# Wide and narrow products on TensorE: three narrow products a weight tile in place of one wide and one narrow, new score order and pads in the attention phase

## Chip, cores and metric

The kernel runs on one core of a Trainium2 chip. The metric is the device time of one execution in microseconds; the time before is the median of three runs. The core's engines are TensorE (PE; its weight loads are shown as PEld), VectorE (DVE), ScalarE (ACT), GpSimd (POOL) and SyncE (SP, which issues the loads).

## What is computed

A decoder trunk of two layers on `x` of 256 positions by 2048 features, float32. Layer 0 is a sliding-window attention with 32 query heads and 8 key/value heads of 64 features, norms of q and k over the head, and a learned sink per head. Layer 1 is a recurrent block (RG-LRU). Each is followed by a gated MLP with a causal depthwise convolution (FFN) of 6144 hidden features.

```python
for layer in range(DEPTH):
    h = rmsnorm(x, mix_norm[layer])
    if layer % N_MIXERS == 0:
        x = x + sliding_window_attention(h, attn_w_qkv[j], attn_q_gain[j], attn_k_gain[j], attn_sinks[j], attn_w_o[j])
    else:
        x = x + rglru_block(h, rec_w_in[j], ..., rec_w_out[j])
    h = rmsnorm(x, ffn_norm[layer])
    x = x + conv_ffn(h, ffn_w_up[layer], ffn_conv_w[layer], ffn_conv_b[layer], ffn_w_down[layer])
```

`conv_ffn` is `u = dwconv(h @ w_up)`, split into `g` and `v`, then `(gelu(g) * v) @ w_down`. `rglru_block` projects by `w_in` to two halves, convolves one, forms two gates from it by block-diagonal matrices, runs a linear recurrence over positions, multiplies by gelu of the other half and projects by `w_out`.

## The kernel before

Everything is transposed: features lie on the 128 partitions, the 256 positions along the free axis (`T = 256`, `KD = 16` tiles of features). All weights come in chunks of 128 x 2048 float32 (1 MB), 376 of them, in one order fixed in `order`: 4 for k, 4 for v, 16 for q, 16 for wo, then FFN 0 (two halves, each 48 chunks up and 24 down), 32 for the recurrent projections `px` and `py`, 16 for the output projection, FFN 1. A chunk is 16 weight tiles of 128 x 128.

**Precision.** Products run in float32r. To keep float32 accuracy, each operand is split in two, high and low. A weight chunk gets `hi` (a rounded copy by ACT, `split_hi`, line 118) and `lo` (the rest, by DVE, `split_lo`, line 126). An activation tile holds both parts side by side: `h[:, k, 0, :]` high, `h[:, k, 1, :]` low, 256 columns each; `g`, `ao`, `z` and `xc` are made likewise. A product needs hi by x-high, hi by x-low and lo by x-high.

**Wide and narrow.** A PSUM bank holds 512 columns. A *wide* product multiplies a `hi` tile with both parts at once, 512 columns, so the left half of the bank gathers hi by x-high and the right half hi by x-low. A *narrow* product multiplies a `lo` tile with x-high, 256 columns, into the right half. A chunk is 16 wide and 16 narrow products. The consumer adds the halves: in the FFN ACT copies the left half (`ua`, line 738), DVE adds the right (`us`, line 739) and multiplies by the norm's factor (line 740); `projected` does the same in the recurrent stage (lines 810 to 812); the residual update `x_epi` takes two adds (lines 234, 235), and `q_epi` a copy, an add, then cast, square and subtraction (lines 514 to 518).

**Order of the products.** `products` (line 213) issues for each chunk a counted run of wide products, some left over from the chunk before, then the chunk's 16 narrow ones. The counts come from `counts` (line 223): 14, 16, 18 at a stage's head, then 15, 15, 18 over and over, and at a stage's end all that is left. `mm_hi` and `mm_lo` (lines 190 to 199) issue 16 wide and 16 narrow in turn: so in the recurrent projections, the attention phase and `late_pair`, the first two chunks behind a norm.

**Queues.** `advance` issues the next chunk's load on SP (three raw buffers), then `split_hi` on ACT and `split_lo` on DVE; the code places it behind each chunk's products, between the steps of the previous tile's epilogue (`step`, `finish`). Each engine works its queue in the order written.

**Attention rounds.** `attend(j)` issues query tile j's products in pieces, and between them, in this order: the values product of tile j-3 (`O`, nine narrow products, line 605), the scores of tile j-1 (`scores`, line 521) and the transposes of tile j-2's probabilities in two halves of three (line 587). `scores` issues first the four float32 products that sum the squares of q (line 527, which need `qsq`), then for the second block of queries four products of 512 columns (mask by an identity, then hi by low, low by high, hi by high: lines 533 to 536), then four of 256 for the first block. `wo` begins with three tiles d = 0 to 2 that are interleaved with the last rounds; their update `wo_epi` follows at line 698. d = 3 to 15 run as plain chunks through `products`.

**Addresses.** A pool lays its tiles out in the order in which they are first asked for, at multiples of 32 bytes a partition. By the tiles' sizes, `hi` and `lo` start 64 bytes past a multiple of 512 and `h`, `g`, `ao`, `z`, `xc`, `kz` and `vh` 128 past. The gates' weights `ghi` and `glo` start 128 past, `identr`, `maskr`, the transposed probabilities `pt` and the query tiles `qh` 32 past.

Of the kernel before, what the change touches and what calls it, by code (L numbers as in the profile page):

```python
# [19 lines left out]
F32 = mybir.dt.float32  # L20
# [20 lines left out]
def trunk(ctx, tc, xT, wq, wk, wv, wo, win, wg, wout, wup, wdn, mixg, ffng, kqg, sinks,  # L41
# [158 lines left out]

    left = []

    def hi_items(ps, hi, rhs, ks, off=0, n=P, start=True):
        return [[ps, hi[:, off + k * n:off + k * n + P], rhs[:, xk].rearrange("p a t -> p (a t)"),
                 start and k == ks[0][0], False] for k, xk in ks]

    def lo_items(ps, lo, rhs, ks, off=0, n=P, stop=True):
        return [[ps[:, T:], lo[:, off + k * n:off + k * n + P], rhs[:, xk, 0, :], False,  # L210
                 stop and k == ks[-1][0]] for k, xk in ks]

    def products(high, low, count):

        run = left + high
        count = len(run) if count is None else count
        left[:] = run[count:]
        if left and low[-1][4]:
            low[-1][4], left[-1][4] = False, True
        for ps, w, r, start, stop in run[:count] + low:  # L220
            pe.matmul(ps, lhsT=w, rhs=r, start=start, stop=stop)  # L221

    def counts(n):

        c = ([14, 16, 18] + [15, 15, 18] * (n // 3))[:n]
        c[-1] = None
        return iter(c)

    def x_epi(ps, d, n, gains, tp, out_=None, tag="xt"):

        t = tp.tile([P, n, T], F32, tag=tag, name=f"xt{st['use']}")
        xs = x[:, d:d + n, :]
        for i in ([slice(0, n)] if out_ is None else [slice(i, i + 1) for i in range(n)]):
            dve.tensor_tensor(out=t[:, i], in0=ps[:, i, 0:T], in1=xs[:, i], op=ALU.add)  # L234
            dve.tensor_tensor(out=xs[:, i], in0=ps[:, i, T:], in1=t[:, i], op=ALU.add)  # L235
            if out_ is not None:
                nc.sync.dma_start(out=out_[:, d:d + n, :][:, i], in_=xs[:, i])
# [76 lines left out]
    with ExitStack() as ph:  # L314
# [6 lines left out]

        kz = ap_.tile([P, 4, 2, 2, T], F32R, name="kz")
        vh = ap_.tile([P, 2, 2, 512], F32R, name="vh")
        ao = ap_.tile([P, KD, 2, T], F32R, name="ao")
# [4 lines left out]
        cb = ap_.tile([P, T], F32, name="cb")  # L329
# [3 lines left out]
        rcv = ap_.tile([P, 2], F32, name="rcv")  # L333
        bones = ap_.tile([P, P], F32, name="bones")
        ident = ap_.tile([P, P], F32, name="ident")
        identr = ap_.tile([P, P], F32R, name="identr")
        maskf = a2.tile([P, 2, T], F32, tag="pt", padded_shape=[P, 2, 768], name="maskf")
        maskr = ap_.tile([P, 2, T], F32R, name="maskr")
# [170 lines left out]
        def q_epi(j, ps):  # L509
            a = a2.tile([P, T], F32, tag="ka", name=f"qa{j}")  # L510
            s = a2.tile([P, T], F32, tag="ks", name=f"qs{j}")
            sq = a2.tile([P, T], F32, tag="ksq", name=f"qsq{j}")
            ql = a2.tile([P, 2, T], F32R, tag="qh", name=f"qh{j}")
            act.copy(out=a, in_=ps[:, 0:T])
            dve.tensor_tensor(out=s, in0=ps[:, T:], in1=a, op=ALU.add)
            act.copy(out=ql[:, 0, :], in_=s)
            act.activation(out=sq, in_=s, func=AF.Square)
            dve.tensor_tensor(out=ql[:, 1, :], in0=s, in1=f(ql[:, 0, :]), op=ALU.subtract)
            qs[j] = (ql, sq)

        def scores(j):
# [4 lines left out]
            for b in range(2):  # L526
                pe.matmul(pq[:, 2 * b:2 * b + 2], lhsT=sq[:, b * P:b * P + P], rhs=bones[:, 0:P:HD],
                          start=True, stop=True)
            for b, o, keys in ((1, S[:, 0:512].rearrange("p (a t) -> p a t", a=2), slice(0, T)),
                               (0, S[:, 512:768].rearrange("p (a t) -> p a t", a=2), slice(0, P))):  # L530
                tb = slice(b * P, b * P + P)
                mk = slice(0, T) if b else slice(P, T)
                pe.matmul(o, lhsT=identr, rhs=maskr[:, :, mk], start=True, stop=False)
                pe.matmul(o, lhsT=ql[:, 0, tb], rhs=kz[:, p, 1, :, keys], start=False, stop=False)
                pe.matmul(o, lhsT=ql[:, 1, tb], rhs=kz[:, p, 0, :, keys], start=False, stop=False)
                pe.matmul(o, lhsT=ql[:, 0, tb], rhs=kz[:, p, 0, :, keys], start=False, stop=True)
# [80 lines left out]
        def attend(j, ps, hi, lo, rhs, nk, fin=None):  # L617


            sm = None  # L620
            dma_next()
# [11 lines left out]
            mm_hi(ps, hi, rhs, rng(8, 10), start=False)  # L633
            if j >= 2:
                transposes(j - 2, 0)
            mm_hi(ps, hi, rhs, rng(10, 13), start=False)
            if j >= 2:
                transposes(j - 2, 1)
            mm_hi(ps, hi, rhs, rng(13, nk), start=False)
# [3 lines left out]
            mm_lo(ps, lo, rhs, rng(0, nk), stop=nk == KD)  # L643
# [20 lines left out]
        head = []  # L664
# [387 lines left out]
```

## Time and profile before

| | |
|---|---|
| median of 3 runs | 2178.98 us (2178.93 to 2179.07) |
| the profiled execution | 2179.0 us, of which span 2177.2 us |
| products on PE | 12676, busy 2162.8 us |
| DVE, ACT, POOL busy | 72%, 54%, 7% |
| HBM read | 401.06 MB, 185 GB/s over the span |

The profile is of one execution. Its page gives busy time by engine, a chain of work followed back from the last instruction, and groups of instructions by line with busy time, mean duration and the idle time ahead of them. Its other views are the waits, each with who ended it, and the timeline, in which equal instructions that follow each other form one row: start, duration, engine, line, operation, tiles, shape and count. A product's own duration is its way through the array and overlaps with the next one's. The pace at which products follow each other is read from the starts. `pu`, `pd`, `pr`, `px`, `py`, `pq`, `po` are the PSUM tiles of the FFN's up and down products, the output projection, the recurrent projections, the queries and wo.

### The profile page before, as it was taken

The numbers are of one execution on the slowest core, as the hardware profiler recorded it, in microseconds if no ns is written. First come the engines' busy times: TensorE is split into PE (matmuls) and PEld (weight loads), VectorE is DVE, ScalarE is ACT, GpSimd is POOL, SyncE is SP. The second block draws the span as 40 slices with busy tenths as digits, with TensorE's granted clock in tenths as the row PEclk, the third lists the DMA queues.
The fourth block names the chain that finished last, engine by engine and source line by source line (L and its number), as shares of the span: only waits on it lengthen the run. The fifth ranks groups of instructions, "written<-read, shape, count | busy, mean of one in ns | idle before, by whom it ended". The sixth has DMA issues, their size and how long they took to land.

```text
span 2177.2 us, 30752 instructions
## 1 busy us (share of the span) xinstructions
PE 2162.8 (99%) x12676; PEld 1899.5 (87%) x12676; DVE 1567.5 (72%) x1882; ACT 1174.0 (54%) x1432; POOL 143.6 (7%) x125
## 2 busy tenths in 40 slices
PE   9999999999999999999999999999999999999999
PEld 7878888888888888888888988888888888888888
DVE  6778777777654777776679877777776457777654
ACT  6777445555433555553369874555554335555432
POOL 1222220000000000002200003200000000000000
PEclk9999999999999999999999999999999999999999
DMA  7223555555555555555555546555555555555553
GB/s 274 104 102 112 193 188 199 195 192 194 193 193 194 185 192 191 191 193 195 189 213 186 191 151 214 185 196 194 192 192 196 188 186 191 193 192 193 192 195 135
DMA packets 60763, 405.14 MB, mean 186 GB/s; under 512 B 7504, under 2 KB 9936, under 8 KB 12880
## 3 DMA queue, kind: packets, MB, share of 16 engines
q1 hardware_dynamic: 60336, 403.04, 52.0%
q8 instruction: 99, 1.62, 0.3%
q14 instruction: 40, 0.33, 0.0%
q10 hardware_dynamic: 288, 0.15, 0.0%
HBM read 401.06 MB, written 2.10 MB: 185 GB/s over the span
## 4 chain that ended last, share of the span: by engine, by line
PE 94%; ACT 3%; DVE 2%; issue 1%; DMA 0%; SPq 0%; DVEq 0%; ACTq 0%
PE pu L221 47%; PE pd L221 24%; PE pr L221 4%; PE po L221 3%; PE py L192 3%; PE px L192 3%; PE px L198 1%; PE py L198 1%; PE pq L192 1%; ACT pr L565 1%; ACT hi L118 1%; PE pu L192 1%; PE pq L198 1%; DMA x<-in_xT 0%; PE po L192 0%
## 5 line engine op out<-in xcount | busy, mean ns | idle before, releaser
L126 DVE TENSOR_TENSOR lo<-raw,hi 128x2048 fp32r<-128x2048 f32 (+1 forms) x390 | 863.1, 2214 | 299.6 <-ACT hi L118 299.5
L118 ACT CAST hi<-raw 128x2048 fp32r<-128x2048 f32 x373 | 712.9, 1912 | 493.4 <-PE pd L221 220.8
L221 PE MATMUL pu<-h,hi 128*128 128x512 f32 x3008 | 719.1, 391 | 0.0
L221 PEld LDWEIGHTS pu<-h,hi 128*128 128x128 f32 x3008 | 551.0, 188 | 107.6
L221 PEld LDWEIGHTS pu<-h,lo 128*128 128x128 f32 x3008 | 369.7, 188 | 16.1
L221 PE MATMUL pu<-h,lo 128*128 128x256 f32 x3008 | 372.4, 276 | 0.0
L221 PE MATMUL pd<-g,hi 128*128 128x512 f32 x1536 | 367.3, 391 | 0.0
L221 PEld LDWEIGHTS pd<-g,hi 128*128 128x128 f32 x1536 | 281.4, 188 | 55.0
L221 PEld LDWEIGHTS pd<-g,lo 128*128 128x128 f32 x1536 | 188.9, 188 | 8.2
L221 PE MATMUL pd<-g,lo 128*128 128x256 f32 x1536 | 190.3, 276 | 0.0
L747 DVE SCALAR_TENSOR_TENSOR uy<-us,fw,uy 128x255 f32<-128x255 f32 (+1 forms) x384 | 176.6, 481 | 6.8
L754 ACT CAST g<-us 128x256 fp32r<-128x256 f32 x96 | 39.1, 407 | 246.2 <-DVE us L753 246.2
L739 DVE TENSOR_TENSOR us<-pu,ua 128x512 f32<-128x512 f32 x96 | 66.4, 691 | 88.9 <-ACT ua L738 88.8
L744 ACT ACTIVATE uy<-us,fb,fw 128x256 f32<-128x256 f32 x192 | 105.1, 599 | 2.7 <-DVE us L740 2.7
L738 ACT COPY ua<-pu 128x512 f32<-128x512 f32 x96 | 56.4, 587 | 77.6 <-PE pu L221 77.6
L192 PE MATMUL pq<-h,hi 128*128 128x512 f32 x256 | 73.7, 405 | 0.0
L755 DVE TENSOR_TENSOR g<-us,g 128x256 fp32r<-128x256 f32 x96 | 40.9, 426 | 45.4 <-ACT g L754 45.4
L740 DVE TENSOR_TENSOR us<-us,rb 128x512 f32<-128x512 f32 x96 | 66.4, 692 | 3.3
L161 POOL TENSOR_TENSOR sqa<-x 128x512 f32<-128x512 f32 x3 | 6.9, 2300 | 897.5 <-DVE x L235 897.5
L192 PE MATMUL px<-h,hi 128*128 128x512 f32 x256 | 61.8, 392 | 0.0
L192 PE MATMUL py<-h,hi 128*128 128x512 f32 x256 | 61.3, 392 | 0.0
L234 DVE TENSOR_TENSOR xt<-pd,x 128x512 f32<-128x512 f32 (+1 forms) x40 | 23.3, 582 | 50.3 <-PE pd L221 50.3
(226 smaller groups left out, 1925.7 us busy)
## 6 DMA issues: line engine op xcount, KB each, us to landing
raw<-in_wup SPq DMA_DIRECT2D x192, 1024.0 KB, 4.8
raw<-in_wdn SPq DMA_DIRECT2D x96, 1024.0 KB, 4.8
raw<-in_win SPq DMA_DIRECT2D x32, 1024.0 KB, 4.9
raw<-in_wq SPq DMA_DIRECT2D x16, 1024.0 KB, 4.8
raw<-in_wo SPq DMA_DIRECT2D x16, 1024.0 KB, 4.8
raw<-in_wout SPq DMA_DIRECT2D x16, 1024.0 KB, 4.7
raw<-in_wv SPq DMA_DIRECT2D x4, 1024.0 KB, 5.7
graw<-in_wg SPq DMA_DIRECT2D x8, 512.0 KB, 3.4
```

What stands on the lines that cost most here:

```text
L118: act.copy(out=his[c], in_=raws[c])
L126: dve.tensor_tensor(out=los[c][:, part], in0=raws[c][:, part], in1=f(his[c][:, part]), op=ALU.subtract)
L192: pe.matmul(ps, lhsT=hi[:, off + k * n:off + k * n + P], rhs=rhs[:, xk].rearrange("p a t -> p (a t)"), start=start and k == ks[0][0], stop ...
L198: pe.matmul(ps[:, T:], lhsT=lo[:, off + k * n:off + k * n + P], rhs=rhs[:, xk, 0, :], start=False, stop=stop and k == ks[-1][0])
L221: pe.matmul(ps, lhsT=w, rhs=r, start=start, stop=stop)
L738: act.copy(out=a, in_=ps[:, :, 0:T])
L739: dve.tensor_tensor(out=s, in0=ps[:, :, T:], in1=a, op=ALU.add)
L740: dve.tensor_tensor(out=s, in0=s, in1=rbb, op=ALU.mult)
L744: act.activation(out=y[:, i, :], in_=s[:, i, :], func=AF.Identity, scale=fw[:, layer, n, 2:3], bias=fb[:, layer, n:n + 1])
L747: dve.scalar_tensor_tensor(out=y[:, i, tap:], in0=s[:, i, 0:T - tap], scalar=fw[:, layer, n, 2 - tap:3 - tap], in1=y[:, i, tap:], op0=ALU. ...
L754: act.copy(out=g[:, m, 0, :], in_=s[:, 0, :])
L755: dve.tensor_tensor(out=g[:, m, 1, :], in0=s[:, 0, :], in1=f(g[:, m, 0, :]), op=ALU.subtract)
```

## The change

Outside the products behind k and v and `late_pair`, the wide product goes: each `hi` tile is multiplied with x-high and with x-low in two narrow products, and both, like the `lo` tile's, go into the left half of the bank. `two_hi` issues the 32 narrow products of a chunk's `hi` tiles, `one_lo` the 16 of its `lo` tiles. The consumers read one half: no copy and add in `q_epi`, one add in `x_epi`, only the multiply in `up_epi` and `projected` (through `whole`).

At the head of a stage, `begin(n)` keeps n chunks in the old form: 15 wide products each (those left over first), then the chunk's 16 narrow ones; behind the last of them what is left is issued as narrow halves. n is 3 for wo from d = 3, for each down half and for the recurrent projections, and 4 for each up half and the output projection. The tiles of these chunks are still joined from two halves.

`scores` now issues the second block's scores as two groups of four narrow products, one per head of the pair, then the squares' sums, then the first block's four; in each group low by high comes last. In the attention pool the small tiles move ahead of `vh`, and pads are put between; with them `vh`, `identr` and `qh` start 64 bytes past a multiple of 512 and `ao`, `maskr` and `pt` 128 past, with the tag `ks` gone. In the gates' pool pads of 448 and 64 bytes put `ghi` and `glo` at 64 and leave `xc` at 128.

```diff
+    def two_hi(ps, hi, rhs, ks, off=0, n=P, start=False):
+        for k, xk in ks:
+            for part in range(2):
+                pe.matmul(ps, lhsT=hi[:, off + k * n:off + k * n + P], rhs=rhs[:, xk, part, :],
+                          start=start and (k, part) == (ks[0][0], 0), stop=False)
+    def one_lo(ps, lo, rhs, ks, off=0, n=P, stop=True):
+        for k, xk in ks:
+            pe.matmul(ps, lhsT=lo[:, off + k * n:off + k * n + P], rhs=rhs[:, xk, 0, :], start=False,
+                      stop=stop and k == ks[-1][0])
+    def thirds(ps, hi, lo, rhs, ks, off, n, start, stop):
+        two_hi(ps, hi, rhs, ks, off, n, start)
+        one_lo(ps, lo, rhs, ks, off, n, stop)
+    head = {"n": 0, "left": []}
+    def begin(n):
+        head["n"] = n
+    def chunk(*items):
+        if not head["n"]:
+            for ps, *rest in items:
+                thirds(ps[:, 0:T], *rest)
+            return False
+        head["n"] -= 1
+        high, low = list(head["left"]), []
+        for ps, hi, lo, rhs, ks, off, n, start, stop in items:
+            for k, xk in ks:
+                w = slice(off + k * n, off + k * n + P)
+                high.append((ps, hi[:, w], rhs, xk, start and k == ks[0][0], stop))
+                low.append((ps, slice(T, 2 * T), lo[:, w], rhs[:, xk, 0, :], False, stop))
+        ops = [(ps, slice(0, 2 * T), w, rhs[:, xk].rearrange("p a t -> p (a t)"), first, stop)
+               for ps, w, rhs, xk, first, stop in high[:15]] + low
+        left = high[15:]
+        if not head["n"]:
+            ops += [(ps, slice(part * T, part * T + T), w, rhs[:, xk, part, :], False, stop)
+                    for ps, w, rhs, xk, first, stop in left for part in range(2)]
+            left = []
+        head["left"] = left
...
+        return True
...
+    def whole(s, ps, tp, two, name):
+        rbb = rb.unsqueeze(1).to_broadcast([P, 2, T])
+        if two[0]:
+            i = slice(0, 1 + two[1])
+            a = tp.tile([P, 2, T], F32, tag="a", bufs=1, name=name)
+            act.copy(out=a[:, i], in_=ps[:, i, 0:T])
+            dve.tensor_tensor(out=s[:, i], in0=ps[:, i, T:], in1=a[:, i], op=ALU.add)
+            dve.tensor_tensor(out=s[:, i], in0=s[:, i], in1=rbb[:, i], op=ALU.mult)
+        if not two[1]:
+            i = slice(int(two[0]), 2)
+            dve.tensor_tensor(out=s[:, i], in0=ps[:, i, 0:T], in1=rbb[:, i], op=ALU.mult)
...
     def x_epi(ps, d, n, gains, tp, out_=None, tag="xt", two=False):
...
-            dve.tensor_tensor(out=t[:, i], in0=ps[:, i, 0:T], in1=xs[:, i], op=ALU.add)
-            dve.tensor_tensor(out=xs[:, i], in0=ps[:, i, T:], in1=t[:, i], op=ALU.add)
+            if two:
+                dve.tensor_tensor(out=t[:, i], in0=ps[:, i, T:], in1=xs[:, i], op=ALU.add)
+            dve.tensor_tensor(out=xs[:, i], in0=ps[:, i, 0:T], in1=t[:, i] if two else xs[:, i], op=ALU.add)
...
         def q_epi(j, ps):
...
-            act.copy(out=a, in_=ps[:, 0:T])
-            dve.tensor_tensor(out=s, in0=ps[:, T:], in1=a, op=ALU.add)
-            act.copy(out=ql[:, 0, :], in_=s)
-            act.activation(out=sq, in_=s, func=AF.Square)
-            dve.tensor_tensor(out=ql[:, 1, :], in0=s, in1=f(ql[:, 0, :]), op=ALU.subtract)
+            act.copy(out=ql[:, 0, :], in_=ps[:, 0:T])
+            act.activation(out=sq, in_=ps[:, 0:T], func=AF.Square)
+            dve.tensor_tensor(out=ql[:, 1, :], in0=ps[:, 0:T], in1=f(ql[:, 0, :]), op=ALU.subtract)
...
         def scores(j):
...
-            for b in range(2):
-                pe.matmul(pq[:, 2 * b:2 * b + 2], lhsT=sq[:, b * P:b * P + P], rhs=bones[:, 0:P:HD],
-                          start=True, stop=True)
-            for b, o, keys in ((1, S[:, 0:512].rearrange("p (a t) -> p a t", a=2), slice(0, T)),
-                               (0, S[:, 512:768].rearrange("p (a t) -> p a t", a=2), slice(0, P))):
+            for b, o, m, kk in ((1, S[:, 0:256], maskr[:, 0], (0, slice(0, T))),
+                                (1, S[:, 256:512], maskr[:, 1], (1, slice(0, T))),
+                                (0, S[:, 512:768].rearrange("p (a t) -> p a t", a=2), maskr[:, :, P:],
+                                 (slice(0, 2), slice(0, P)))):
                 tb = slice(b * P, b * P + P)
...
+                pe.matmul(o, lhsT=identr, rhs=m, start=True, stop=False)
+                pe.matmul(o, lhsT=ql[:, 0, tb], rhs=kz[:, p, 1, kk[0], kk[1]], start=False, stop=False)
+                pe.matmul(o, lhsT=ql[:, 0, tb], rhs=kz[:, p, 0, kk[0], kk[1]], start=False, stop=False)
+                pe.matmul(o, lhsT=ql[:, 1, tb], rhs=kz[:, p, 0, kk[0], kk[1]], start=False, stop=True)
+                if kk[0] == 1:
+                    for c in range(2):
+                        pe.matmul(pq[:, 2 * c:2 * c + 2], lhsT=sq[:, c * P:c * P + P], rhs=bones[:, 0:P:HD],
+                                  start=True, stop=True)
...
         def attend(j, ps, hi, lo, rhs, nk, fin=None):
...
-            mm_hi(ps, hi, rhs, rng(0, 4))
+            two_hi(ps, hi, rhs, rng(0, 2), start=True)
             if j >= 3:
                 ao_split(j - 3, values(j - 3))
-            mm_hi(ps, hi, rhs, rng(4, 8), start=False)
+            two_hi(ps, hi, rhs, rng(2, 6))
             if 1 <= j <= 16:
                 S = scores(j - 1)
...
-            mm_lo(ps, lo, rhs, rng(0, nk), stop=nk == KD)
+            one_lo(ps, lo, rhs, rng(0, nk), stop=nk == KD)
...
+                if n == 0:
+                    gw.tile([P, 112], F32, name="gpad0")
                 hi = gw.tile([P, 1024], F32R, tag="ghi", name=f"ghi{n}")
                 lo = gw.tile([P, 1024], F32R, tag="glo", name=f"glo{n}")
+                if n == 0:
+                    gw.tile([P, 16], F32, name="gpad1")
```

More of the change, by code (lines that the diff above doesn't have):

```diff
@@ L780, in ffn @@
                         ks = [(kk, 8 * c + kk) for kk in range(8)]
-                        high, low = [], []
-                        for i in range(2):
-                            high += hi_items(ps[:, i], hi, g, ks, off=i * P, n=2 * P, start=c == 0)
-                            low += lo_items(ps[:, i], lo, g, ks, off=i * P, n=2 * P, stop=c == 2)
-                        products(high, low, next(runs))
+                        two = chunk(*((tiles[i], hi, lo, g, ks, i * P, 2 * P, c == 0, c == 2) for i in range(2)))
                         step(pend)
```

154 lines of the change are left out of this document (67 added, 87 removed).

## The prediction

> **What bounds the kernel.** I read the page first: busy shares, granted clock, chain.
>
> ```profile
> span 2177.2 us, 30752 instructions
> PE 2162.8 (99%) x12676; PEld 1899.5 (87%) x12676; DVE 1567.5 (72%) x1882; ACT 1174.0 (54%) x1432; POOL 143.6 (7%) x125
> ...
> PEclk9999999999999999999999999999999999999999
> ...
> PE 94%; ACT 3%; DVE 2%; issue 1%; DMA 0%; SPq 0%; DVEq 0%; ACTq 0%
> ...
> L739 DVE TENSOR_TENSOR us<-pu,ua 128x512 f32<-128x512 f32 x96 | 66.4, 691 | 88.9 <-ACT ua L738 88.8
> ...
> L738 ACT COPY ua<-pu 128x512 f32<-128x512 f32 x96 | 56.4, 587 | 77.6 <-PE pu L221 77.6
> ```
>
> TensorE is the bound: 99% busy at full clock in every slice, 94% of the chain. The profiled execution took 2179.0 us, 1.8 of it outside the span, and the median of the runs is 2178.98, so sums made on the profile stand for the runs. Since a busy PE is not a PE at its peak, the question is at what pace products start. The timeline of PE gives that: it merges a run of equal products into a row, so the start of the next row minus the start of this one, divided by the count, is the pace.
>
> ```profile
> 567.50 3.38 PE L221 MATMUL pd<-g,hi 128*128 128x512 f32 x14
> ...
> 600.45 3.60 PE L221 MATMUL pd<-g,hi 128*128 128x512 f32 x15
> 603.88 1.98 PE L221 MATMUL pd<-g,lo 128*128 128x256 f32 x16
> 605.69 3.60 PE L221 MATMUL pd<-g,hi 128*128 128x512 f32 x15
> 609.12 1.98 PE L221 MATMUL pd<-g,lo 128*128 128x256 f32 x16
> 610.94 4.28 PE L221 MATMUL pd<-g,hi 128*128 128x512 f32 x18
> 615.06 1.98 PE L221 MATMUL pd<-g,lo 128*128 128x256 f32 x16
> 616.87 3.60 PE L221 MATMUL pd<-g,hi 128*128 128x512 f32 x15
> ...
> 699.00 3.36 PE L221 MATMUL pu<-h,hi 128*128 128x512 f32 x14
> 702.21 2.05 PE L221 MATMUL pu<-h,lo 128*128 128x256 f32 x16
> 704.09 3.83 PE L221 MATMUL pu<-h,hi 128*128 128x512 f32 x16
> ...
> 962.08 3.36 PE L221 MATMUL pd<-g,hi 128*128 128x512 f32 x14
> ```
>
> Around 600 us the 48 wide products take 3.43 + 3.43 + 4.12 = 10.98 us, 228.8 ns each, and the 48 narrow ones 1.81 + 1.82 + 1.81 = 5.44 us, 113.3 ns each. Two narrow products (226.7) are thus cheaper than one wide one (228.8). A chunk costs (10.98 + 5.44)/3 = 5.473 us; as 48 narrow products at that pace it would cost 5.440. The second point is at 702: the same kind of narrow run, at a stage's head, takes 1.88 us, 117.5 ns each. So a narrow run has two paces, 113.3 and 117.5, and every run keeps the one it starts with. Over 303 chunks the difference is 303 x 48 x 4.2 ns = 61 us. The whole question is which pace an unbroken narrow stream keeps.
>
> **The steady chunks.** The change replaces 16 wide + 16 narrow products by 48 narrow ones into one half of a bank. Outside the attention rounds, the unchanged late pairs and the chunks behind k and v, 303 chunks get this form and 38 stand in the heads. I take 113.3 ns: the operands lie at the same offsets as in the narrow runs above, whose weights walk through all of a chunk while the pace stays put. A head of 15 wide products a chunk is a multiple of three; the runs behind 15, 15 and 18 wide products at 600 are the good ones, the run behind 14 at 702 is a bad one. So I read the heads as bringing PE into the good pace, which it then keeps, no stall following: of FFN, recurrent stage and output projection the waits of PE show nothing.
>
> One up half (699.00 to 962.08, 48 chunks, 263.08 us) becomes 44 x 5.440 plus a head of 60 wide and 72 narrow products, 13.73 + 8.16: 261.25, so -1.8; four halves, two of them 46 chunks: -7.1. A down half (567.50 to 699.00, 131.50) becomes 21 x 5.440 + 45 x 0.2288 + 54 x 0.1133 = 130.66: -0.85, four of them -3.4. Both ends of the pace are kept for the range.
>
> A rule of the Trainium skill speaks against this: "TensorE: Matmul & The Clock Gate", section "Back-to-back issue gap", gives N/2.4 + 2.5 ns a product once warm, a fixed part that splitting a wide product pays twice. By it a chunk gains 16 x 2.5 = 40 ns instead of losing 33. The two paces above fit no such fixed part on the good side (2 x 113.3 is below 228.8) and one of 6.2 ns on the bad side (2 x 117.5 - 228.8), so the measured rows go into the sum.
>
> The copies and adds that joined two halves (L738 587 ns, L739 691 ns a tile pair) go from ACT and DVE except in heads. I cost that at nothing: in the FFN PE waits for neither. The multiply by the norm then reads PSUM itself, as L739 does now. Loads and their order on SP's queue stay.
>
> **Recurrent stage, gates, projections.** Rows, here also for the attention part:
>
> ```profile
> 55.97 3.83 PE L192 MATMUL pq<-h,hi 128*128 128x512 f32 x16
> ...
> 163.25 0.61 PE L527 MATMUL S<-bones,qsq 128*128 128x2 f32 x4 [1.16 <-ACT qsq L517]
> ...
> 172.53 0.61 PE L527 MATMUL S<-bones,qsq 128*128 128x2 f32 x4
> ...
> 181.81 0.59 PE L527 MATMUL S<-bones,qsq 128*128 128x2 f32 x4
> ...
> 228.56 2.15 PE L198 MATMUL po<-ao,lo 128*128 128x256 f32 x16 [0.39 <-DVE lo L126]
> 230.55 3.37 PE L221 MATMUL po<-ao,hi 128*128 128x512 f32 x14
> 234.93 2.15 PE L221 MATMUL po<-ao,lo 128*128 128x256 f32 x16 [1.01 <-DVE lo L126]
> ...
> 303.33 3.38 PE L192 MATMUL pu<-h,hi 128*128 128x512 f32 x14
> ...
> 1105.64 3.83 PE L192 MATMUL px<-h,hi 128*128 128x512 f32 x16
> ...
> 1122.24 0.28 PE L861 MATMUL g<-xc,ghi 128*128 128x256 f32 x1
> ...
> 1125.12 2.22 PE L192 MATMUL px<-h,hi 128*128 128x512 f32 x9
> ...
> 1294.25 3.38 PE L192 MATMUL pr<-z,hi 128*128 128x512 f32 x14
> ...
> 1305.36 3.37 PE L221 MATMUL pr<-z,hi 128*128 128x512 f32 x14
> ...
> 1382.26 3.38 PE L192 MATMUL pu<-h,hi 128*128 128x512 f32 x14
> ```
>
> The 24 gate products (1122.24 to 1125.12) run at 120.0 ns. They are narrow like the others; what differs is that by the order and sizes of the tiles their weights and their moving operand both start 128 bytes past a multiple of 512, while hi and lo start 64 past and h, g, z, ao 128 past. The pads of 448 and 64 bytes put ghi and glo at 64, so I take 113.3 for them too; if the offset isn't the reason, 192 x 6.7 ns = 1.3 us come back. From 1105.64 to 1294.25 (188.61) it becomes 27 x 5.440 + 10.30 + 6.12 + 192 x 0.1133 = 185.06: -3.5. Output projection, 1305.36 to 1382.26 (76.90): 10 x 5.440 + 21.89 = 76.29: -0.6. Projection wo, 230.55 to 303.33 (72.78): 54.40 + 16.42 = 70.82, -2.0 if the wait of 1.01 goes. That wait is for DVE, which had joined two tiles with two adds each; I take -1.8.
>
> **Attention rounds.** Two chains change.
>
> ```profile
> PE S L527 <- ACT qsq L517: 4.6, 5, 1.2
> PE O L605 <- DVE pt L592: 1.5, 3, 0.7
> ```
>
> ```profile
> 161.24 0.35 ACT L514 COPY qa<-pq 128x256 f32<-128x256 f32 x1
> 162.48 0.40 ACT L516 CAST qh<-qs 128x256 fp32r<-128x256 f32 x1 [0.88 <-DVE qs L515]
> 162.79 0.41 ACT L517 ACTIVATE qsq<-qs 128x256 f32<-128x256 f32 x1
> ```
>
> Now ACT copies one half (161.24), waits 0.88 for DVE's add, and only then casts and squares, while PE stands at its score products until 163.25. Without copy and add the cast can start at 161.24, 1.2 us sooner, about the longest wait; and the products on the squares move behind eight score products. So the five waits on qsq, 4.6 us, go. What is late next is pt, DVE's share of the transposed probabilities, 1.5 us in three waits; with 0.4 us less DVE work a round I count half of it gone. Against it: here the stream is cut by the sums of squares and transposes in every round, so no head keeps it in step. The run behind a wait at 228.56 (1.99 us for 16, restart included) is of the slow kind. A round without a wait takes 9.28 us (172.53 to 181.81); with 48 + 9 + 12 narrow products at 117.5 in it instead of 113.3 it is up to 0.3 longer, at 113.3 some 0.1 shorter. Of 14 full rounds: +4 to -1.4; I take +1.3, since the narrow runs here are of both kinds now. Together -4 (-7.5 to +4), from 55.97 to 230.55.
>
> **The tail.**
>
> ```profile
> 2172.73 0.42 DVE L234 TENSOR_TENSOR xt<-pd,x 128x256 f32<-128x256 f32 x1 [12.56 <-PE pd L221]
> ...
> 2173.98 0.42 DVE L235 TENSOR_TENSOR x<-pd,xt 128x256 f32<-128x256 f32 x1
> ```
>
> Four adds stand between the last product and the last output transfer, ending at 2174.40; two remain: -0.8.
>
> **Sum:** 7.1 + 3.4 + 3.5 + 0.6 + 1.8 + 4 + 0.8 = 21.2 us, less 0.2 for narrow runs in the heads before the pace is caught: 2179.0 - 21.0 = 2158.0. With the bounds of attention (-3.5, +8) and of the gates (+1.3) and an uncertainty of 4 below for waits in the wo head and pt, this case lies between 2150 and 2167.
>
> **Rivals.** (1) The narrow stream settles at 117.5, because the good pace needs the wide runs in between: each chunk then gives 48 x 4.2 ns more, 2158 + 61 = 2219, slower by 1.8%. It decides from 114.0 ns on, where 48 narrow products cost the 5.473 of now. For it: the head runs and the run behind a wait. Against: no run changes pace inside, and two thirds of each chunk's time at 600 are already in step with it. The page's rule would end here too, near 2180, by its estimate of 40 ns a chunk. (2) Some stages fall out of step behind a short wait after their head: an up half then loses 44 x 48 x 4.2 ns = 8.9 us; one to three such stages give 2167 to 2185. Against: no such waits now, and ACT and DVE get lighter. (3) The instructions don't come fast enough: a chunk needs 96 (weight load and product each) instead of 64, where PE now gets 64 in 5.473 us, 85.5 ns each, and in the longest narrow stretch, a narrow run with 24 gates behind it, about 60. At 60 a chunk is 5.76: 2158 + 303 x 0.32 = 2255; at 85.5 far more. The same page's section "Wait — 56ns, not 53.3ns?" names 62 ns a product for a decode in microcode; no run here shows which decode is on.
>
> **How the numbers follow.** Forecast 0.70; rival 1 0.10; rival 2 0.15; rival 3 0.05. A measurement of this kernel can tell about 0.2% (4.4 us) from no change. The forecast is all faster. Of rival 2 I give 0.06 to faster (below 2174.6), 0.06 to the same and 0.03 to slower; rivals 1 and 3 are slower: 0.76, 0.06, 0.18. The range 2150 to 2178 takes in the forecast's own range and most of rival 2, leaving out rivals 1 and 3 and the end of rival 2, 0.18.
>
> **What would show it.** In the timeline of the changed kernel: rows of 48 and more narrow products at 113.3 ns behind each head, gates at 113.3, an up half of 261 us, the wait of S on qsq gone from the waits of PE, and no wait of PE in the FFN. Narrow rows at 117.5 in a whole stage would mean rival 2, in all of them rival 1; a pace that falls only after some tens of products, rival 3.

## The result, and the profile after

| | before | after |
|---|---|---|
| median | 2178.95 us (2178.66 to 2179.07, 4 runs) | 2154.57 us (2152.51 to 2156.38, 4 runs) |
| profiled execution, and its span | 2179.0, 2177.2 us | 2152.51, 2150.7 us |

The ratio is 0.9888, 95% interval 0.9871 to 0.9905: 1.1% faster, 24.4 us against the 21.0 forecast. From the page of the changed kernel:

```profile
PE 2144.2 (100%) x17930; PEld 2104.3 (98%) x17930; DVE 1459.9 (68%) x1715; ACT 1125.7 (52%) x1317; POOL 140.4 (7%) x125
```

PE issues 5254 more products and is done sooner; the weight loads now fill 98% of the span, while DVE and ACT have less to do. The waits of PE:

```profile
...
PE po L209 <- DVE lo L126: 0.3, 1, 0.3
PE O L650 <- DVE pt L637: 0.2, 1, 0.2
```

The waits of the scores (4.6 us before) are gone, of the values product 0.2 of 1.5 is left. The waits left out lie ahead of the query products. The timeline of PE follows, with the starts of the stages (L204 is `two_hi`, L209 `one_lo`, L250 a chunk in a head). These rows, here and below, come from short windows: a duration and a count can stop at the window's end, so only the starts are compared.

```profile
56.67 1.58 PE L204 MATMUL pq<-h,hi 128*128 128x256 f32 x12
...
137.01 0.28 PE L574 MATMUL S<-maskr,identr 128*128 128x256 f32 x1
...
146.01 0.28 PE L574 MATMUL S<-maskr,identr 128*128 128x256 f32 x1
...
221.23 3.60 PE L250 MATMUL po<-ao,hi 128*128 128x512 f32 x15
...
292.35 1.99 PE L192 MATMUL pu<-h,hi 128*128 128x512 f32 x8
...
554.79 3.60 PE L250 MATMUL pd<-g,hi 128*128 128x512 f32 x15
...
571.21 1.98 PE L204 MATMUL pd<-g,hi 128*128 128x256 f32 x16
...
573.93 1.98 PE L204 MATMUL pd<-g,hi 128*128 128x256 f32 x16
...
685.45 3.60 PE L250 MATMUL pu<-h,hi 128*128 128x512 f32 x15
...
946.71 3.60 PE L250 MATMUL pd<-g,hi 128*128 128x512 f32 x15
...
1089.27 3.60 PE L250 MATMUL px<-h,hi 128*128 128x512 f32 x15
...
1105.86 0.28 PE L901 MATMUL g<-xc,ghi 128*128 128x256 f32 x1
...
1108.58 3.68 PE L204 MATMUL px<-h,hi 128*128 128x256 f32 x31
...
1274.50 3.37 PE L192 MATMUL pr<-z,hi 128*128 128x512 f32 x14
...
1285.53 3.60 PE L250 MATMUL pr<-z,hi 128*128 128x512 f32 x15
...
1361.82 3.37 PE L192 MATMUL pu<-h,hi 128*128 128x512 f32 x14
```

From 571.21 to 573.93 lie 24 narrow products in 2.72 us, 113.3 ns each; the 24 gates from 1105.86 to 1108.58 take 2.72 us too, 113.3 instead of 120.0. Stage by stage, worked out from these starts and those shown before:

| stage | before | forecast | after | change |
|---|---|---|---|---|
| attention rounds and start of wo | 174.58 | 170.6 | 164.56 | -10.0 |
| wo, from d = 3 | 72.78 | 71.0 | 71.12 | -1.7 |
| up half (second) | 263.08 | 261.25 | 261.26 | -1.8 |
| down half (first) | 131.50 | 130.66 | 130.66 | -0.8 |
| recurrent projections and gates | 188.61 | 185.06 | 185.23 | -3.4 |
| output projection | 76.90 | 76.29 | 76.29 | -0.6 |

One row is far from its forecast: the attention rounds. Behind the last product two adds are left of the four:

```profile
2147.04 0.76 DVE L260 TENSOR_TENSOR x<-pd,x 128x256 f32<-128x256 f32 x2 [12.99 <-PE pd L209]
```

The other thing not foreseen is the scatter. Eight executions of this kernel lie between 2152.4 and 2156.4 us, with steps of about 2, where the kernel before stays within 0.4 in the four runs beside it (over all comparisons in this study it lay between 2178.5 and 2180.2, without such steps).

### The profile page after: what moved, and what is told of

Same layout as the page of the kernel before. It is cut to its first block, busy times and chain, and to the rows that moved or that the text cites. A ratio compares the mean times of both kernels' runs of the same rounds, so it can differ in the third digit from the quotient of the medians.

```text
span 2150.7 us, 40983 instructions
## 1 busy us (share of the span) xinstructions
PE 2144.2 (100%) x17930; PEld 2104.3 (98%) x17930; DVE 1459.9 (68%) x1715; ACT 1125.7 (52%) x1317; POOL 140.4 (7%) x125
## 4 chain that ended last, share of the span: by engine, by line
PE 97%; DVE 1%; DMA 1%; ACT 1%; issue 0%; DVEq 0%; ACTq 0%
PE pu L204 29%; PE pu L209 15%; PE pd L204 14%; PE pd L209 7%; PE pu L250 4%; PE pd L250 3%; PE py L204 3%; PE pq L204 2%; PE po L204 2%; PE px L204 2%; PE pr L204 2%; PE py L209 1%; PE po L209 1%; PE pr L250 1%; PE pq L209 1%; PE px L209 1%
## 5 line engine op out<-in xcount | busy, mean ns | idle before, releaser
L204 PE MATMUL pu<-h,hi 128*128 128x256 f32 x5504 | 651.8, 276 | 0.0
L204 PEld LDWEIGHTS pu<-h,hi 128*128 128x128 f32 x5504 | 636.6, 188 | 0.0
L209 PE MATMUL pu<-h,lo 128*128 128x256 f32 x2752 | 339.9, 276 | 0.0
L204 PE MATMUL pd<-g,hi 128*128 128x256 f32 x2688 | 332.0, 276 | 0.0
L209 PEld LDWEIGHTS pu<-h,lo 128*128 128x128 f32 x2752 | 324.7, 188 | 0.0
L204 PEld LDWEIGHTS pd<-g,hi 128*128 128x128 f32 x2688 | 317.1, 188 | 0.0
L209 PE MATMUL pd<-g,lo 128*128 128x256 f32 x1344 | 179.6, 276 | 0.0
L209 PEld LDWEIGHTS pd<-g,lo 128*128 128x128 f32 x1344 | 164.8, 188 | 0.0
L288 DVE TENSOR_TENSOR us<-pu,rb 128x512 f32<-128x512 f32 x86 | 59.5, 692 | 149.5 <-PE pu L209 149.5
L204 PE MATMUL pq<-h,hi 128*128 128x256 f32 x512 | 73.9, 284 | 0.0
L204 PEld LDWEIGHTS pq<-h,hi 128*128 128x128 f32 x512 | 64.6, 188 | 0.2
L250 PE MATMUL pu<-h,hi 128*128 128x512 f32 (+1 forms) x272 | 61.9, 378 | 0.0
L204 PE MATMUL py<-h,hi 128*128 128x256 f32 x512 | 60.6, 276 | 0.0
L204 PEld LDWEIGHTS py<-h,hi 128*128 128x128 f32 x512 | 59.2, 188 | 0.0
```

What stands on the lines that cost most here:

```text
L204: pe.matmul(ps, lhsT=hi[:, off + k * n:off + k * n + P], rhs=rhs[:, xk, part, :], start=start and (k, part) == (ks[0][0], 0), stop=False)
L209: pe.matmul(ps, lhsT=lo[:, off + k * n:off + k * n + P], rhs=rhs[:, xk, 0, :], start=False, stop=stop and k == ks[-1][0])
L250: pe.matmul(ps[:, cols], lhsT=w, rhs=rhs, start=first, stop=stop and last.get(id(ps)) == i)
L288: dve.tensor_tensor(out=s[:, i], in0=ps[:, i, 0:T], in1=rbb[:, i], op=ALU.mult)
```

## The experiments

The theory: a narrow run has a good pace of 113.3 ns and a slow one of 117.8, keeps the one it enters with; the length of the wide run ahead of it, modulo three, decides which; and the good one needs weights and moving operand at different offsets in 512 bytes. The rivals: lighter ACT and DVE made the gain; any narrow stream runs at 113.3; offsets have nothing to do with it.

**The same kernel once more.**

> The changed kernel once more, unaltered. Its four times so far lie at 2152.5, 2154.6, 2154.6 and 2156.4 us, in steps of about 2 us, where the kernel before stays within 0.4. Theory (two paces of a narrow run, 113.3 and 117.5 to 117.8 ns, and a run keeps the one it enters with): the steps are short stretches of the attention phase or of wo that enter the one or the other pace, so this profile has the same stage times from the first up half on (261.25 us an up half, 130.66 a down half) and differs only ahead of it. Rival: the clock or the loads vary, and all stages differ a little.

Measured: median 2152.78 us (2152.37 to 2154.49), ratio 0.988 (0.9865 to 0.9895). In its profile each stage from the first up half on has the time of the first profile to 0.01 us or so. The 2 us steps did not fall into this profiled execution; three later profiles, of edits elsewhere, show one source of them: wo took 73.34 to 73.41 us there instead of 71.12.

**Heads.** No head at all; and heads of 14.

```diff
-        begin(3)
+        begin(0)
```

with the same at all five places, and

```diff
-               for ps, w, rhs, xk, first, stop in high[:15]] + low
-        left = high[15:]
+               for ps, w, rhs, xk, first, stop in high[:14]] + low
+        left = high[14:]
```

> No chunk of a stage's head is kept wide: all are narrow from the first. Theory (heads set the pace, a narrow stream keeps it): in the changed kernel the last narrow products of the late pairs ahead of up 0, of the recurrent projections and of up 1 are at 118 ns, those ahead of the output projection at 113. Without heads the first three stay slow up to the next wide run: 142 + 142 + 30 chunks of 48 products, 4.45 ns each, 67 us, gates 0.9 us, less 1.5 us of the heads' own cost: 2154.6 + 66 = 2221, with the output projection at 113.3 throughout. Rival (any narrow stream runs at 113.3, heads only cost): 2153.

> Heads of 14 wide products a chunk in place of 15, what is left over goes to the end of the head as before. The work is the same. Theory (the pace behind a wide run depends on its length modulo three): behind 14 no run is brought into the good pace for good; it leaves heads at 117.8 in all stages, some 303 chunks x 48 x 4.45 ns = 65 us and a little in the heads: 2221. Rival (heads give time to other engines, or nothing at all): 2155, no stage different.

Heads of 14: 2220.57 us (2220.39 to 2220.89), ratio 1.019 (1.0173 to 1.0207), 0.4 us from the expectation. One wide product less in each chunk of a head costs 66 us. The timeline of PE around its first down half's head:

```profile
569.27 1.98 PE L250 MATMUL pd<-g,lo 128*128 128x256 f32 x16
571.08 3.37 PE L250 MATMUL pd<-g,hi 128*128 128x512 f32 x14
574.28 2.05 PE L250 MATMUL pd<-g,lo 128*128 128x256 f32 x16
576.17 3.38 PE L250 MATMUL pd<-g,hi 128*128 128x512 f32 x14
...
582.68 2.05 PE L204 MATMUL pd<-g,hi 128*128 128x256 f32 x16
...
585.51 2.05 PE L204 MATMUL pd<-g,hi 128*128 128x256 f32 x16
```

The narrow run at 569.27 takes 1.81 us (113 ns each). Fourteen wide products later the run at 574.28 takes 1.89 (118), and the stream behind the head keeps that: 24 in 2.83 us, 117.9 ns. The other stages are slow too: the second up half takes 271.03 us, a down half 135.34. That any narrow stream runs at 113.3 is out.

The rows also limit the theory. The good run at 569.27 itself stands behind 14 wide products, which followed a slow stream. And in the changed kernel a head of 15 does not work at once; this is the one of the recurrent projections, from the wide run at 1089.27 on:

```profile
1092.70 2.05 PE L250 MATMUL px<-h,lo 128*128 128x256 f32 x16
1094.59 0.63 PE L250 MATMUL px<-h,hi 128*128 128x512 f32 x2
...
1103.37 1.98 PE L250 MATMUL px<-h,lo 128*128 128x256 f32 x16
1105.18 0.84 PE L250 MATMUL px<-h,hi 128*128 128x256 f32 x6
```

The 16 narrow products behind the first 15 wide ones take 1.89 us, those behind the second 1.88, and only those behind the third 1.81. Over the traces of the changed kernel and its variants with weights and moving operand 64 bytes apart (12 in all; wide runs between narrow runs of at least eight), all 203 runs of 15 that were entered in the good pace left in it, and all 41 runs of 14 with an unbroken narrow run behind them lost it. Entered in the slow pace, 26 of 55 runs of 15 led to the good one. So the length decides for a stream that is in step; what brings a slow one in step, and why sometimes only the third run does, stays open.

Without heads the four executions fall into two groups: the profiled one took 2215.4 us, the others 2163.8 to 2165.2, against 2221 expected for all; the granted clock was 0.999 to 1.000 in all four. The profiled one ran both FFNs slow:

```profile
601.88 2.05 PE L204 MATMUL pd<-g,hi 128*128 128x256 f32 x16
...
604.71 2.05 PE L204 MATMUL pd<-g,hi 128*128 128x256 f32 x16
```

24 in 2.83 us again, 117.9, and this over all 142 chunks of each FFN; wo was slow too, the recurrent stage in the good pace, not the slow one as expected. The other three must have run most of it in the good pace, which no trace shows. So I took the heads out of one part at a time.

> Heads taken out in the FFN alone, kept in wo, the recurrent projections and the output projection. With no heads anywhere the profiled execution ran all 284 FFN chunks at 117.8 ns (2215 us), while three other executions took 2164. Theory as it stands: the late pairs end slow ahead of up 0 and up 1, so both FFNs stay slow in each execution: 284 x 48 x 4.45 ns = 61 us less 1.5 for heads, 2153 + 59 = 2212. Rival A (the entry differs from one execution to another, and the three fast ones entered the FFNs in the good pace): 2151 to 2152 in some executions, 2182 or 2212 in others. Rival B (a slow stream is knocked into the good pace by some event): values anywhere between.

> Heads taken out in wo, the recurrent projections and the output projection, kept in the FFN. Theory: wo is slow as without any heads, 13 x 0.21 = +2.8; the late pair ahead of the recurrent projections ends slow, so 30 chunks and the gates are slow, +7.3; the output projection is entered in the good pace; heads saved 0.5: 2153 + 9.6 = 2163. That would be the 2164 of three executions without any heads, with both FFNs good. Rival (only wo is slow): 2155.

Without heads in the FFN: 2212.22 us (2210.94 to 2213.57), ratio 1.015 (1.0135 to 1.0165), all four slow as the theory has it. In its profile wo, whose head stayed, is slow as well (73.41 us). Without them in wo, recurrent and output projections: 2164.51 (2164.31 to 2165.03), ratio 0.9931 (0.9917 to 0.9946); its profile has wo, recurrent stage and output projection at 117.8 and the FFN untouched. The expectation, 2163, had the output projection good; it follows a slow stage here and stays slow; presumably its late pair of chunks, whose wide run should bring it in step, is entered differently; this is not shown. The time is that of the three shorter executions without any heads, which fits good FFNs in them. Why these missed the slow pace in the FFN stays open: without a head the entry is left to what the stage before leaves behind, and that differed.

**Offsets.** Gates' pads out, and the weight chunks at the moving operands' offset.

```diff
-                    gw.tile([P, 112], F32, name="gpad0")
-                    gw.tile([P, 16], F32, name="gpad1")
```

```diff
     sp8 = per.tile([P, KD], F32, name="sp8")
+    per.tile([P, 16], F32, name="perpad")
-    gap.tile([P, 16], F32, name="pad")
```

> The two pads in the gates' pool are taken out, so the gates' weights and moving operand start at the same offset in 512 bytes again, as in the kernel before. Theory (the offset between weights and moving operand sets the pace): gates at 120.0 ns instead of 113.3, 192 x 6.7 ns = 1.3 us: 2156; and if the stream behind the gates resumes in the slow pace, up to 26 chunks x 0.21 us = 5.5 us more: 2161. Rival (the gates gained by following narrow products instead of wide ones): 2154.6 and gates at 113.3.

> The weight chunks (raw, hi, lo) are moved by 64 bytes, so that their weights start 128 bytes past a multiple of 512 like the moving operands h, g, z and ao; all other tiles stay where they are. Theory (the good pace needs weights and moving operand at different offsets; the gates at equal offsets run at 120.0 ns): all narrow runs of the plain chunks at 120.0 ns, 303 x 48 x 6.7 ns = 97 us more and some 5 in heads and attention: about 2255, an up half at 277 us. Rival (the 120 ns belong to the gates' short groups, not to the offset): 2153.

Gates' pads out: 2153.79 us (2153.0 to 2155.99), ratio 0.9885 (0.987 to 0.99), which the timing alone can't tell from the changed kernel. The timeline can:

```profile
1105.36 0.28 PE L901 MATMUL g<-xc,ghi 128*128 128x256 f32 x1
...
1108.24 3.79 PE L204 MATMUL px<-h,hi 128*128 128x256 f32 x32
```

24 gates in 2.88 us, 120.0 ns; the stage takes 186.51 us against 185.23, 1.28 more, as 192 x 6.7 ns. The stream behind them comes back to 113.3, so the larger expectation falls.

Weight chunks moved: 2255.58 us (two runs, 2255.53 and 2255.62), ratio 1.035 (1.0329 to 1.0371), against an expectation of 2255. Nothing but an address has changed. Its timeline:

```profile
602.61 2.08 PE L204 MATMUL pd<-g,hi 128*128 128x256 f32 x16
...
605.49 2.08 PE L204 MATMUL pd<-g,hi 128*128 128x256 f32 x16
```

24 in 2.88 us, 120.0 ns each, in all plain stages, while its gates, still at 64 against 128, run at 113.3. At equal offsets the runs lie at 119 to 120 ns with heads and without, so heads don't help. Other distances than 64 bytes were not tried for the chunks.

**ACT and DVE loaded again.** Where tiles are read from one half, a copy and a second pass come back:

```diff
+            b = tp.tile([P, 2, T], F32, tag="a", bufs=1, name=name + "b")
+            act.copy(out=b[:, i], in_=ps[:, i, 0:T])
+            dve.tensor_tensor(out=s[:, i], in0=ps[:, i, 0:T], in1=b[:, i], op=ALU.max)
-            dve.tensor_tensor(out=s[:, i], in0=ps[:, i, 0:T], in1=rbb[:, i], op=ALU.mult)
+            dve.tensor_tensor(out=s[:, i], in0=s[:, i], in1=rbb[:, i], op=ALU.mult)
```

> The copy on ACT and a second pass on DVE are put back where up tiles and recurrent tiles are read from one half (a maximum of the tile with its own copy in place of the add, so values stay as they are): ACT gets some 0.59 us and DVE 0.69 us a tile pair, as before the change. PE's products are those of the changed kernel. Theory (the gain in the FFN is PE's pace alone): no difference beyond 1 us, 2152 to 2155, up half 261.25 us. Rival (lighter ACT and DVE let PE run without small waits): a part of the 10.6 us of the FFN and the 3.4 of the recurrent stage comes back, 2156 to 2168.

Measured: 2159.56 us (2159.16 to 2160.77), ratio 0.9909 (0.9894 to 0.9924), 5.0 us more than the changed kernel by the medians, 8.3 by the profiled executions; I had expected no difference beyond 1 us. By stages the FFN is as expected, 261.25 us the up half and 130.66 the down half. The loss is elsewhere, as the timeline shows:

```profile
229.84 2.05 PE L250 MATMUL po<-ao,lo 128*128 128x256 f32 x16
231.72 3.61 PE L250 MATMUL po<-ao,hi 128*128 128x512 f32 x15
...
1157.68 1.98 PE L209 MATMUL px<-h,lo 128*128 128x256 f32 x16
1159.49 0.28 PE L904 MATMUL g<-xc,ghi 128*128 128x256 f32 x1
1160.93 0.39 PE L905 MATMUL g<-xc,ghi 128*128 128x256 f32 x1 [1.16 <-DVE xc L873]
...
1257.02 3.93 PE L204 MATMUL py<-h,hi 128*128 128x256 f32 x32
1260.79 2.05 PE L209 MATMUL py<-h,lo 128*128 128x256 f32 x16
```

In the recurrent stage one gate product waited 1.16 us for DVE. Ahead of it 16 narrow products take 1.81 us; a hundred us later 32 take 3.77, 117.8 each, up to the stage's end: 191.24 us against 185.23. The wait itself is a fifth of the 6.0 us; the rest is the lost pace. This is the mechanism of the second rival, at a place where the changed kernel doesn't wait. And wo, whose code is the same, left its head slow (16 in 1.88 us at 229.84): 73.34 us against 71.12. Its head's first chunk waits for `lo`, and presumably this shifts where the next wide run begins; this is not shown.

**wo's head, and fewer heads.** `begin(4)` for wo instead of `begin(3)`; then, besides, heads left only in wo, the recurrent projections and the first up half of each FFN.

```diff
-        begin(3)
+        begin(4)
```

```diff
-                        if m == (half == 0):
+                        if t == 1:
                             begin(4)
...
-                begin(3)
+                begin(0)
                 for dp in range(8):
...
-                    begin(4)
+                    begin(0)
```

> One more chunk in the head of wo, four instead of three. In the execution with the loads put back, wo stayed slow behind its head (73.34 us against 71.11 in the changed kernel), though its code was the same: a wait for the low weights falls into the head's first chunk, and its length decides in which step the next wide run starts; two more chunks are not always enough. Theory: with a fourth chunk wo leaves its head in the good pace in each execution: the 2 us steps between executions of the changed kernel go, all at 2152.5 plus or minus 0.5. Rival (the steps come from elsewhere): 2152 to 2156 as before.

> Heads only where the stage is entered in the slow pace: wo (4 chunks), the recurrent projections (3), the first up half of each FFN (4). Down halves, second up halves and the output projection have none. Theory (a stream keeps its pace from stage to stage where nothing waits): all those stages at 5.440 us a chunk from the first, 261.12 us an up half without a head and 130.56 a down half, 0.8 us less in all than with four chunks in wo: about 2151.7. Rival (a stage's start itself throws PE out of step): slow stages, +4 to +9 us each.

Four in wo: 2152.97 us (2152.18 to 2153.41), ratio 0.9879 (0.9864 to 0.9893). Four runs with no step of 2 us fit the theory; three of the changed kernel's eight are at 2152.5 too, so that the step is gone is likely, not shown; the four executions below, with the same head in wo, have none either. Fewer heads: 2151.69 us (2151.39 to 2152.12), ratio 0.9873 (0.9859 to 0.9888), 2151.7 expected. The starts of its second up half and of the down half behind it:

```profile
685.13 3.79 PE L204 MATMUL pu<-h,hi 128*128 128x256 f32 x32
...
946.25 1.98 PE L204 MATMUL pd<-g,hi 128*128 128x256 f32 x16
```

261.12 us, 48 x 5.440: the stream goes from stage to stage without a head. It is the fastest kernel here, though its interval overlaps that of the change.

**Attention.** The old chain of the query tiles; and the squares' sums ahead of the scores.

```diff
+            s = a2.tile([P, T], F32, tag="ka", name=f"qa{j}")
+            act.copy(out=s, in_=ps[:, 0:T])
+            dve.tensor_tensor(out=s, in0=ps[:, 0:T], in1=s, op=ALU.max)
-            act.copy(out=ql[:, 0, :], in_=ps[:, 0:T])
-            act.activation(out=sq, in_=ps[:, 0:T], func=AF.Square)
-            dve.tensor_tensor(out=ql[:, 1, :], in0=ps[:, 0:T], in1=f(ql[:, 0, :]), op=ALU.subtract)
+            act.copy(out=ql[:, 0, :], in_=s)
+            act.activation(out=sq, in_=s, func=AF.Square)
+            dve.tensor_tensor(out=ql[:, 1, :], in0=s, in1=f(ql[:, 0, :]), op=ALU.subtract)
```

```diff
+            for c in range(2):
+                pe.matmul(pq[:, 2 * c:2 * c + 2], lhsT=sq[:, c * P:c * P + P], rhs=bones[:, 0:P:HD],
+                          start=True, stop=True)
             for b, o, m, kk in ((1, S[:, 0:256], maskr[:, 0], (0, slice(0, T))),
```

> In the attention rounds the old chain of the query tiles is put back: copy by ACT, a pass by DVE (a maximum with the copy instead of the add), then cast, square and subtraction. Order of scores, narrow products and pads stay. Theory (the shorter chain ended the waits for the squares): PE waits again in the scores, by less than the 4.6 us of before since the squares now come 8 products (0.9 us) later, and attention loses 2 to 5 us: 2155 to 2158. Rival (the rounds gained by the pace and the order of products alone): 2153 to 2154 with no wait.

> The sums of squares go back to the front of the scores, as before the change; the short chain of the query tiles stays. Theory (the shorter chain alone ended the waits): the squares are done about 0.8 us behind the last product of a tile and the scores come 2.4 us behind it, so PE waits for nothing, up to 1 us lost: 2153 to 2154. Rival (their place behind eight products also counts): waits for the squares return, 2155 to 2158.

The old chain: 2162.45 us (2162.2 to 2162.84), ratio 0.9922 (0.9906 to 0.9939), more than either expectation. From the first query product to d = 3 of wo it takes 174.74 us against 174.58 before the change: the whole gain of the rounds is gone, though products, order and pads are those of the change. Waits of PE:

```profile
PE S L578 <- ACT qh L561: 2.4, 5, 0.7
PE O L653 <- DVE pt L640: 2.2, 3, 0.9
```

The waits are back, now on the cast, and the values product waits again too. They sum to 4.6 us, about half of the loss. The rest shows in the timeline of a round whose wait is too short for that list:

```profile
191.34 0.28 PE L579 MATMUL S<-kz,qh 128*128 128x256 f32 x1
191.58 0.39 PE L580 MATMUL S<-kz,qh 128*128 128x256 f32 x1
191.81 0.28 PE L577 MATMUL S<-maskr,identr 128*128 128x256 f32 x1
```

Two products in a row start 0.24 and 0.23 us after the one ahead, twice the usual 0.115. The first of them (L580) is low by high, the first product to need the low half of q; the second (L577) multiplies the mask by the identity, needs nothing of q, and comes late behind it. Together they cost 0.24 us. The pace behind them is not worse: the products of this round from the squares on take 8.08 us, against 8.09 in a quiet round of the changed kernel. Both kernels issue the same 1415 products in this stretch, so their starts can be set side by side: 43 late starts of 0.05 us and more, all in the scores and the values products, make 9.7 of the 10.2 us; all the other intervals together add 0.4. So the old chain costs waiting and restarting, some of it too short for the list, and hardly any pace; the chain alone, with nothing else changed, is worth as much as the whole gain of attention.

The squares first: 2155.06 us (2153.89 to 2156.4), ratio 0.9887 (0.987 to 0.9903). No wait on the squares stands in its profile. That execution has wo slow (73.35 us), which this edit doesn't touch, and takes 166.05 us in attention, where the ten profiles with the new order and the short chain lie between 164.50 and 164.60: 11 of its 16 values products of nine take 1.06 us, 117.8 ns a product, against 3 in the changed kernel. So their place costs no listed wait but 1.5 us, mostly by the pace, in this one profile. With the scatter of 2 us in wo the medians can't show it.

## Why the prediction was right, and where it was off

- **The pace of the stream**, the step on which all hung: right. The longest unbroken stretch, 2136 narrow products behind the second up half's head, keeps 113.3 ns to its end. With that the sums of the plain stages came out within 0.2 us of the trace. Heads and offsets, which the forecast only inferred from the runs behind 15 and 14 wide products and from the gates, are now shown by an edit each. How a head works was read too simply: in a slow stream a run of 15 need not bring the good pace. That three chunks sufficed in the recurrent stage, where only the third did, is in part luck; in wo they did not suffice in three of the profiles.
- **The first rival** (117.5 everywhere) is what heads of 14 make: 2220.6, its forecast time 2219. **The second** (falling out of step behind a wait) is what the loaded kernel shows, 6 us for a wait of 1.16. Both are real, and the changed kernel avoids them in both its profiles.
- **The third** (instructions too slow) is out: the stretch above takes 242 us at 4272 instructions, 56.7 ns each. The Trainium skill's "TensorE: Matmul & The Clock Gate", section "Wait — 56ns, not 53.3ns?", gives 62 ns a product for decode in microcode, with decode in hardware off; by an estimate that lets a weight load cost as much, the stretch would take 265 us, so decode at that price doesn't bound this stream.
- **The rule against the change**, 2.5 ns fixed per product in the Trainium skill's "TensorE: Matmul & The Clock Gate", section "Back-to-back issue gap", fell on the wrong side: two narrow products stayed 2 ns cheaper than one wide one. The section gives that formula for a single isolated product, and says itself that a stream of weight loads and products has another spacing, so it was no rule for this stream.
- **ACT and DVE at no cost**: right in the FFN, to 0.01 us an up half. Not right in general: in the recurrent stage the same load makes one wait and costs 6 us. The forecast gave only the FFN as its ground; DVE has less slack in the recurrent stage.
- **Attention** is the term that was mis-sized: -10.0 for -4, beyond its own bound of -7.5. The waits went as the forecast has it, 4.6 + 1.3 instead of 4.6 + 0.75. The step that failed is the round without a listed wait: put at +1.3 us over 14 rounds, it takes 9.00 us (137.01 to 146.01) instead of 9.28, which is 3.9 less over 14. I had read 9.28 as a round without any stall and only asked for its pace. The rows below, of that round before (172.53 to 181.81) and then of the one after, give 0.23 of the 0.28:

```profile
172.99 0.48 PE L533 MATMUL S<-maskr,identr 128*128 128x512 f32 x1
...
176.99 2.05 PE L198 MATMUL pq<-h,lo 128*128 128x256 f32 x16
178.88 1.09 PE L192 MATMUL pq<-h,hi 128*128 128x512 f32 x4
179.81 1.24 PE L605 MATMUL O<-pt,vh 128*128 128x256 f32 x9
```

```profile
137.92 0.50 PE L580 MATMUL S<-bones,qsq 128*128 128x2 f32 x4
138.28 0.36 PE L574 MATMUL S<-maskr,identr 128*128 128x256 f32 x1
...
141.82 1.98 PE L209 MATMUL pq<-h,lo 128*128 128x256 f32 x16
143.63 0.62 PE L204 MATMUL pq<-h,hi 128*128 128x256 f32 x4
144.09 1.18 PE L650 MATMUL O<-pt,vh 128*128 128x256 f32 x9
```

The sums of the squares took 0.46 us before (172.53 to 172.99) and take 0.36: ACT had `qsq` ready at 172.47 (L517, begun at 172.06, 0.41 us long), 0.06 us ahead of them, so a stall of about 0.1 us, too short for the list, was hidden there. The 16 `lo` products take 1.81 instead of 1.89. The nine values products take 1.02 (144.09 to 145.11) instead of 1.07 (179.81 to 180.88), with `pt` and `vh` now 64 bytes apart and before 96. The old chain on the new products costs 10.2 us, nearly all of it in such stalls and in the waits. How much of the 0.28 belongs to the order, to the chain and to the pads no run separates.
- **Sum**: outside attention 17.0 us were forecast. The stages give 16.4 and the tail 0.8; 0.7 is lost ahead of the rounds, where the first query product starts at 56.67 instead of 55.97. Attention's 6.0 beyond its term, less these 0.5, is the difference of 5.5 between the forecast and the profiled execution. The median lies 2 us above that execution, by the scatter, which brings it nearer to the forecast; that is luck.

## What to carry to other kernels

Where an engine is busy all the time, read the pace from the starts of equal instructions, run by run: here two paces of one instruction were worth 66 us, all waits of PE less than 10. Before splitting or joining products, look for the place in the trace where the wanted form already runs, and for a place where it runs badly; the difference between the two is the design rule. A stream that holds a good pace only because of how it was entered must be protected from waits, since a wait of a microsecond can cost the pace for the rest of the stage.

## What the runs showed of the hardware

- Narrow products (256 columns, float32r) with a weight load each have three steady paces here: 113.3 and 117.8 ns with weights and moving operand 64 bytes apart in 512, 120.0 with both at the same offset. The gates kept 113.3 in the middle of a stream at 120.0, when only the stream's operands had the same offset.
- Entered in the good pace, a wide run of 15 left in it (203 of 203) and a run of 14 lost it (41 of 41); entered in the slow pace, 15 led to the good one in 26 of 55. A narrow stream kept its pace over 800 us (6818 products at 117.8 ns, no heads in the FFN).
- One wide product (228.8 ns) costs more than two narrow ones at the good pace (226.7) and less than two at the slow one (235.6).
